# Modulation sums of a diffusion trunk: block turns and row sums on VectorE, a small selection matmul on TensorE

## Chip, cores and metric

The kernel runs on one core of a Trainium2 chip. The metric is the device time of one execution in microseconds (us), the median of several runs. All work is in float32; large products are split into a high and a low part that TensorE multiplies in its faster fp32r form, three matmuls for each product.

## What is computed

The reference is a two-layer trunk over 256 latent and 256 context tokens of width 1024. Each layer has an FFN, a token-mixing part and a second FFN, and each of the three is modulated: nine vectors of 1024 values per layer and stream, computed from a conditioning vector.

```python
sc = jax.nn.silu(c);  scc = jax.nn.silu(c_ctx)
mod_x = (sc @ w_mod[l] + b_mod[l]).reshape(b_, N_MOD, 1, D_MODEL)      # N_MOD = 9
mod_h = (scc @ w_mod[l] + b_mod[l]).reshape(N_MOD, 1, D_MODEL)

def adaln_in(s, g_pre, shift, scale):
    return rmsnorm(s, g_pre) * (1 + scale) + shift
def adaln_out(s, y, g_post, gate, weight):
    return s + weight * gate * rmsnorm(y, g_post)
def swiglu(y, wg, wu, wd):
    return (jax.nn.silu(y @ wg) * (y @ wu)) @ wd
```

For sub-layer j the vectors 3j and 3j + 1 are shift and scale, and 3j + 2 is the gate. The change concerns only how `sc @ w_mod` and `scc @ w_mod` are summed over the 1024 rows of `w_mod`.

## The kernel before

**Modulation.** The first two vectors of layer 0 are made at the start on TensorE (`mod_first`). The other 16 (7 of layer 0, 9 of layer 1) are made in halves of 512 columns, 32 halves in all, by the generator `mod_half` (line 345), while the FFNs run. A half loads its 1024 x 512 part of `w_mod` in two blocks of 1 MB (`stage`, line 207), and VectorE multiplies each 128-row slice by the conditioning value of its row and adds it to one of two accumulators, one for each stream: 16 instructions of 128x512 (lines 355 and 357). What is left is the sum over the 128 partitions. Line 367 makes it on TensorE, with a matrix of ones: four matmuls of 256 columns in four strips of 32 output rows. A gate (q % 3 == 2) is then finished by VectorE at lines 375 and 376 as rows of 256 and written to a table in DRAM by four GpSimd DMAs (line 379); its bias and norm weight come by eight small SyncE DMAs (`by_groups`, line 338). A shift or scale has to be turned so that its 1024 values lie along partitions: ScalarE copies the sums out of PSUM (line 383), and two transposes on TensorE follow later (`turn`, line 385, a "flip"), after which `mod_put` (line 322) writes the coefficients.

**Order of the work.** The program order is laid out by a small planner in the kernel's own source. Its clock `clk` is advanced by `tick(n)` by n / 2400 for n matmul columns; tasks are generators in a heap and run when the clock reaches their due time. `step()` (line 401), called after each pair of hidden blocks of an FFN (line 644) and before each pair of token blocks in the first two down phases (line 494), launches one half when the clock has passed the last launch plus `MOD_PACE`. The half's loads and VectorE work are issued at the next tick, its sums `T_MOD` later. At the start of the last down phase of an FFN, `step(len(modq))` (line 505) launches all that are left in the queue; then `drain` waits for those that are needed next. An FFN has 22 hidden blocks in phases of 6, 8 and 8; each phase is gate/up work for pairs of blocks, then a down projection. The queue gets 12 halves before the first FFN, 10 before the second and 10 before the third; the fourth has none.

**Buffers.** All weight blocks, those of `w_mod` included, pass through three staging buffers (`wst`, tag `stg`). A weight block is split by ScalarE (high part, line 240) and VectorE (low part, line 101) into one of three pairs of buffers (`hi`, `lo`), which TensorE holds until it is done with the block. In the last down phase (from line 505) the two blocks of the first column half are loaded and split ahead of the first matmuls, the two of the second column half after those of the first stream's token blocks in program order. The tile framework places every instruction in its engine's queue by its place in the program and by when its inputs are expected; instructions under `high_priority` go ahead. The two accumulators have the tag `a`, two buffers, so a half can't begin before the one before it is summed.

Of the kernel before, what the change touches and what calls it, by code (L numbers as in the profile page):

```python
# [12 lines left out]
F32 = mybir.dt.float32  # L13
F32R = mybir.dt.float32r
AF = mybir.ActivationFunctionType
ALU = mybir.AluOpType
AX = mybir.AxisListType
PSUM = bass.MemoryType.PSUM

P = 128  # L20
# [15 lines left out]


T_SOFT, T_SOFTC, T_TURN, T_POST = 4.5, 3.5, 1.5, 3.0
T_MOD, T_FLIP, MOD_PACE = 15.0, 2.5, 18.0
PACE_IN, PACE_OUT, PACE_DRAIN = 1.8, 1.0, 1.0  # L40
PACE_IN1, PACE_OUT1, PACE_DRAIN1, T_CHAIN, T_LATE = 1.5, 1.2, 1.2, 7.5, 10.5
PHASES = ((0, 6), (6, 8), (14, 8))
# [21 lines left out]
def trunk(ctx: ExitStack, tc: tile.TileContext, x, c, cx, c_ctx, w_mod, b_mod, norm_pre, norm_post,  # L64
          w_gate, w_up, w_down, w_in, w_out, v_gain, w_s, b_s, diff_lambda, diff_subln, swa_sink,
          rope, out):
    nc = tc.nc

    const = ctx.enter_context(tc.tile_pool(name="const", bufs=1))
# [3 lines left out]
    wk = ctx.enter_context(tc.tile_pool(name="wk", bufs=2))  # L73
    sm = ctx.enter_context(tc.tile_pool(name="sm", bufs=4))
# [6 lines left out]
    def nm(s):  # L81
        cnt[0] += 1
        return f"{s}{cnt[0]}"
# [7 lines left out]
    def pc():  # L91
        return psc.tile([P, 512], F32, tag="c", name=nm("pc"))

    def half(s):
        return wk.tile([P, 512], F32, tag="p", name=nm(s), bufs=6)
# [15 lines left out]
    def run_next():  # L111
        due, _, g = heapq.heappop(evq)
        clk[0] = max(clk[0], due)
        busy[0] = True
        d = next(g, None)
        busy[0] = False
        if d is not None:
            later(d, g)

    def tick(n):  # L120
        clk[0] += n / 2400.0
        while evq and not busy[0] and evq[0][0] <= clk[0]:
            run_next()
# [7 lines left out]

        later(delay, run())

    flips = []

    def flip_now():
        while flips:
            flips.pop(0)()

    def drain(tag):  # L140
        while pending.get(tag, 0):
            run_next()
        if tag[0] == "m":
            flip_now()


    ident = const.tile([P, P], F32, name="ident")
    make_identity(nc, ident)
    ones = const.tile([P, P], F32, name="ones")
    nc.vector.memset(ones, 1.0)  # L150
    negh = const.tile([P, 8], F32, name="negh")
    nc.vector.memset(negh, -0.5)
    mask = const.tile([P, 2, P], F32, name="mask")
# [12 lines left out]
    gtab = {(l, j): dr.tile([2, D], F32, name=f"gate{l}{j}") for l in range(DEPTH) for j in range(3)}  # L166
# [40 lines left out]
    def stage(src_list, nk, ncol, slot="stg"):  # L207
        pool = wst if slot == "stg" else wsp
        st = pool.tile([P, 2048], F32, tag=slot, name=nm(slot))
        v = st[:, 0:nk * ncol].rearrange("p (k c) -> p k c", k=nk)  # L210
        for c0, c1, src in src_list:
            nc.sync.dma_start(v[:, :, c0:c1], src.rearrange("(k p) c -> p k c", p=P))
        return v
# [108 lines left out]
    def mod_put(l, q, b, n, src, mid):  # L322
        j, kind = q // 3, q % 3
        dst = coef[:, l, j, kind, b:b + n, :]

        def bc(ap):
            return ap.unsqueeze(2).to_broadcast([P, n, 2])

        bias = bc(bm[:, l, q * KB + b:q * KB + b + n])
        if kind == 0:  # L330
            nc.vector.tensor_tensor(dst, src, bias, op=ALU.add)
            return
        nc.vector.tensor_tensor(mid, src, bias, op=ALU.add)
        nc.vector.scalar_tensor_tensor(dst, mid, 1.0, bc(npre[:, l, j, b:b + n]),
                                       op0=ALU.add, op1=ALU.mult)


    def by_groups(src):
        r = wk.tile([P, 256], F32, tag="sq", name=nm("gr"), bufs=7)
        for j in range(4):  # L340
            nc.sync.dma_start(r[32 * j:32 * j + 32, :],
                              src[256 * (j % 2):256 * (j % 2) + 256].partition_broadcast(32))
        return r

    def mod_half(l, q, hf):
        acc = [wk.tile([P, 512], F32, tag="a", name=nm("acc")) for _ in range(2)]
        c0 = q * D + hf * 512
        for part in range(2):
            v = stage([(0, 512, w_mod[l, part * 512:(part + 1) * 512, c0:c0 + 512])], 4, 512)
            for k in range(4):  # L350
                kk = 4 * part + k
                for st, a in enumerate(acc):
                    sc = sT[:, kk, st:st + 1]
                    if kk == 0:
                        nc.vector.tensor_scalar(a, v[:, k, :], sc, None, op0=ALU.mult)
                    else:
                        nc.vector.scalar_tensor_tensor(a, v[:, k, :], sc, a, op0=ALU.mult,  # L357
                                                       op1=ALU.add)
        gate = q % 3 == 2
        j = q // 3  # L360
        if gate:
            br = by_groups(b_mod[l, c0:c0 + 512])
            gr = by_groups(norm_post[l, j, hf * 512:(hf + 1) * 512])
        yield T_MOD
        t = pc()
        for i in range(4):
            nc.tensor.matmul(t[32 * i:32 * i + 32, 0:256], lhsT=ones[:, 0:32],
                             rhs=acc[i // 2][:, 256 * (i % 2):256 * (i % 2) + 256],
                             start=True, stop=True, tile_position=(0, 32 * i))
        tick(1024)  # L370
        flip_now()
        if gate:

            w = math.sqrt(D) * (1.0 if j == 1 else 0.5)
            nc.vector.tensor_tensor(br, t[:, 0:256], br, op=ALU.add)
            nc.vector.scalar_tensor_tensor(br, br, w, gr, op0=ALU.mult, op1=ALU.mult)  # L376
            for i in range(4):
                f0 = hf * 512 + 256 * (i % 2)
                nc.gpsimd.dma_start(gtab[l, j][i // 2:i // 2 + 1, f0:f0 + 256],  # L379
                                    br[32 * i:32 * i + 1, :])  # L380
            return
        ev = wk.tile([P, 256], F32, tag="sq", name=nm("modev"), bufs=7)
        nc.scalar.activation(ev, t[:, 0:256], AF.Copy)

        def turn():
            u = pc()
            for i in range(2):
                nc.tensor.transpose(u[:, i * P:(i + 1) * P], ev[:, i * P:(i + 1) * P], ident)
            tick(600)
            uv = u[:, 0:256].rearrange("p (i s h r) -> p h i s r", i=2, s=2, h=2)  # L390
            tmp = sm.tile([P, 2, 2, 2], F32, tag="modt", name=nm("modt"))
            for h in range(2):
                mod_put(l, q, 4 * hf + 2 * h, 2, uv[:, h, :, :, 0], tmp[:, h])

        flips.append(turn)

    modq = []

# [77 lines left out]
    def down(l, e, pi, f0, nf, Z, Uh, Ul, order, nxt):  # L476
# [13 lines left out]
        if not final:  # L490
# [13 lines left out]
            return  # L504
        step(len(modq))
        drain(("m", l, j))
        if nxt is not None:
            drain(("m",) + nxt[:2])
# [46 lines left out]
    def ffn(l, e, streams, nxt, first=None, out_order=None):  # L555
# [36 lines left out]
        for pi, (f0, nf) in enumerate(PHASES):  # L592
            Uh = big.tile([P, KB, NT], F32R, tag="Uh", name=nm("Uh"))
            Ul = big.tile([P, KB, NT], F32R, tag="Ul", name=nm("Ul"))
            for fp in range(0, nf, 2):
# [19 lines left out]
                if two:  # L615
                    into = [t[:, 4:8, :].rearrange("p a (b c) -> p (a b) c", b=2)
                            for t in (Uh, Ul)]
                    second = gate_up(l, e, cs + 256, into, True)
                    for s in range(2) if rows else streams:
                        drain(("y", s))  # L620
                        for f, (g_, u_) in ((0, (wg, wu)), (2, second)):
                            if rows:
                                gu = pa()
                                acc3_multi([(gu[:, c0:c0 + 256], rterms(w, s), c0 == 0)
                                            for w, c0 in ((g_, 0), (u_, 256))])
                                task("u", hidden_rows(gu, f, s))
                                continue
                            gus = [pa(), pa()]
                            groups = []
                            for w, c0 in ((g_, 0), (u_, 256)):  # L630
                                for i in range(2):
                                    groups.append((gus[i][:, c0:c0 + 256], yterms(w, i * P, s),
                                                   c0 == 0))
                            acc3_multi(groups)
                            for i in range(2):
                                hidden(gus[i][:, 0:256], gus[i][:, 256:512], f + i, s)
                else:
                    for i in range(2):
                        g = pa()
                        acc3(g[:, 0:n], yterms(wg, i * P, ys))  # L640
                        u = pa()
                        acc3(u[:, 0:n], yterms(wu, i * P, ys))
                        hidden(g[:, 0:n], u[:, 0:n], fp + i, full)
# [581 lines left out]
    acc, ws0 = {}, {}  # L1225
# [57 lines left out]
    def halves(l, *qs):  # L1283
        for q in qs:
            for hf in range(2):
                modq.append((("m", l, q // 3), mod_half(l, q, hf)))
# [42 lines left out]
```

## Time and profile before

| | |
|---|---|
| median of 3 runs | 1762.15 us (1761.32 to 1762.53) |
| profiled execution | 1762.98 us |
| its span, first to last instruction | 1761.2 us |
| TensorE, matmuls | 1722.4 us, 98% of the span |
| VectorE | 1190.4 us, 68% |
| ScalarE | 696.3 us, 40% |
| mean granted clock of TensorE | 0.997 of full speed |

In the profile PE is TensorE's matmuls, PEld its weight loads, DVE is VectorE, ACT ScalarE, POOL GpSimd and SP SyncE, which issues the loads. L367 is line 367 of the kernel. Matmuls overlap, so a matmul's own duration is longer than its share of the stream; the distance between two starts is what counts. In a timeline a row is a start, a duration, the engine, the line, the operation, the tile written and the tiles read, shapes, and how many instructions are merged in the row; what stands in brackets is how long the engine had been idle and what released it.

### The profile page before, as it was taken

Reading aid. Unit: us, or ns where it says so; the run is one execution under the profiler, and the core shown is the slowest. Engines: PE = TensorE matmul, PEld = TensorE weight load, DVE = VectorE, ACT = ScalarE, POOL = GpSimd, SP = SyncE. Lnnn points to the kernel's source line nnn. Section 1 sums busy time; section 2 is a strip of 40 time slices with the busy share of each in tenths; the row PEclk is TensorE's granted clock in tenths of the full one; section 3 lists DMA queues with packets and bytes.
Section 4 is the critical chain, followed back from the end, with each engine's and each line's share of the span. In section 5 each row is a group of like instructions: output and inputs, shape, how many; then the busy total and the mean of one; then the engine's idle time right before and its main releaser. Section 6 shows DMA issues by size and latency. Waiting matters only on the chain.

```text
span 1761.2 us, 24837 instructions
## 1 busy us (share of the span) xinstructions
PE 1722.4 (98%) x9663; PEld 1449.9 (82%) x9663; DVE 1190.4 (68%) x2174; ACT 696.3 (40%) x1480; POOL 168.9 (10%) x185
## 2 busy tenths in 40 slices
PE   7999999999999999999999999999999999999998
PEld 5788888879977789888888898888888897689997
DVE  4876876775667576768766576777864756765555
ACT  4332322244376562333232442332223526655443
POOL 0000000021322120000000210000001321010000
PEclk9999999999999999999999999999999999999999
DMA  9654554543131143445545233655544133226552
GB/s 336 207 173 160 188 197 144 167 150 109 60 103 52 57 137 125 162 163 189 191 144 185 75 120 123 205 178 191 180 144 167 48 108 120 73 90 197 192 191 84
DMA packets 197105, 259.20 MB, mean 147 GB/s; under 512 B 8234, under 2 KB 132348, under 8 KB 196988
## 3 DMA queue, kind: packets, MB, share of 16 engines
q1 hardware_dynamic: 195452, 257.56, 44.3%
q8 instruction: 76, 1.25, 0.3%
q14 instruction: 41, 0.34, 0.1%
q0 software_dynamic: 1536, 0.05, 0.0%
HBM read 256.49 MB, written 1.10 MB: 146 GB/s over the span
## 4 chain that ended last, share of the span: by engine, by line
PE 63%; DVE 7%; ACT 2%; issue 2%; POOL 1%; DMA 1%; POOLq 0%; DVEq 0%; ACTq 0%
PE pa L250 19%; PE pa L254 9%; PE pb L269 4%; PE pb L271 4%; PE pb L263 4%; PE pa L263 4%; PE pa L271 4%; PE pa L269 4%; PE pb L250 3%; DVE lo L101 2%; PE pb L254 1%; PE pa L797 1%; PE pc L818 1%; PE pc L895 1%; DVE S L439 1%
## 5 line engine op out<-in xcount | busy, mean ns | idle before, releaser
L101 DVE TENSOR_TENSOR lo<-stg,hi 128x512 fp32r<-128x512 f32 (+3 forms) x476 | 367.0, 807 | 192.5 <-ACT hi L240 122.8
L240 ACT ACTIVATE hi<-stg 128x512 fp32r<-128x512 f32 (+3 forms) x496 | 318.4, 702 | 329.6 <-PE pa L263 97.2
L250 PE MATMUL pa<-Yh,hi 128*128 128x512 f32 (+1 forms) x1168 | 415.0, 365 | 0.0
L250 PE MATMUL pa<-Yl,hi 128*128 128x512 f32 (+1 forms) x1168 | 413.8, 364 | 0.0
L357 DVE SCALAR_TENSOR_TENSOR acc<-stg,sT,acc 128x512 f32<-128x512 f32 x448 | 305.2, 743 | 4.0 <-DMA stg<-in_w_mod_dram 4.0
L254 PE MATMUL pa<-Yh,lo 128*128 128x512 f32 (+1 forms) x1168 | 257.8, 363 | 0.0
L250 PEld LDWEIGHTS pa<-Yh,hi 128*128 128x128 f32 x1168 | 220.5, 189 | 36.6 <-issue 2.9
L250 PEld LDWEIGHTS pa<-Yl,hi 128*128 128x128 f32 x1168 | 220.5, 189 | 35.0 <-issue 1.2
L254 PEld LDWEIGHTS pa<-Yh,lo 128*128 128x128 f32 x1168 | 202.4, 189 | 34.3
L570 ACT ACTIVATE Uh<-ha 128x512 fp32r<-128x512 f32 (+1 forms) x92 | 50.7, 551 | 296.4 <-DVE ha L568 296.4
L263 PE MATMUL pb<-hi,Ul 128*128 128x512 f32 x400 | 156.9, 392 | 0.0
L271 PE MATMUL pb<-lo,Uh 128*128 128x512 f32 x400 | 155.9, 390 | 0.8 <-DVE lo L101 0.8
L269 PE MATMUL pb<-hi,Uh 128*128 128x512 f32 x400 | 155.8, 391 | 0.1
L568 DVE TENSOR_TENSOR ha<-ha,pa 128x512 f32<-128x512 f32 (+1 forms) x91 | 53.0, 583 | 79.5 <-PE pa L254 79.0
L269 PE MATMUL pa<-Yh,hi 128*128 128x256 f32 x368 | 92.0, 285 | 0.0
L271 PE MATMUL pa<-Yl,hi 128*128 128x256 f32 x368 | 91.3, 283 | 0.0
L271 PEld LDWEIGHTS pb<-lo,Uh 128*128 128x128 f32 x400 | 75.1, 188 | 16.6 <-DVE lo L101 1.3
L263 PEld LDWEIGHTS pb<-hi,Ul 128*128 128x128 f32 x400 | 75.1, 188 | 16.5 <-issue 1.2
L269 PEld LDWEIGHTS pb<-hi,Uh 128*128 128x128 f32 x400 | 75.2, 188 | 16.0 <-DVE Z L503 0.5
L566 ACT ACTIVATE ht<-pa 128x512 f32<-128x512 f32 (+1 forms) x91 | 46.3, 510 | 104.1 <-PE pa L254 81.8
L379 POOL DMA_DIRECT2D gate<-gr x48 | 24.3, 513 | 603.7 <-DVE gr L376 535.3
L567 DVE SCALAR_TENSOR_TENSOR ha<-ht,pa 128x512 f32<-128x512 f32 (+1 forms) x91 | 52.9, 581 | 37.2 <-ACT ht L566 36.4
(299 smaller groups left out, 2732.4 us busy)
## 6 DMA issues: line engine op xcount, KB each, us to landing
stg<-in_w_mod_dram SPq DMA_DIRECT2D x64, 1024.0 KB, 5.0
stg<-in_ffn_w_gate_dram SPq DMA_DIRECT2D x42, 1024.0 KB, 5.2
stg<-in_ffn_w_up_dram SPq DMA_DIRECT2D x42, 1024.0 KB, 5.1
stg<-in_ffn_w_down_dram SPq DMA_DIRECT2D x32, 1024.0 KB, 5.0
stg<-in_w_in_dram SPq DMA_DIRECT2D x14, 1024.0 KB, 4.8
stg<-in_ffn_w_down_dram SPq DMA_DIRECT2D x16, 768.0 KB, 4.4
mst<-in_w_mod_dram SPq DMA_DIRECT2D x16, 512.0 KB, 7.6
stg<-in_w_out_dram SPq DMA_DIRECT2D x8, 1024.0 KB, 6.4
```

The lines of the kernel that those rows point to most:

```text
L101: eng.tensor_tensor(lo, full, f32(hi), op=ALU.subtract)
L240: nc.scalar.activation(hi[:, a:b, :], v[:, a:b, :], AF.Copy)
L250: nc.tensor.matmul(o, lhsT=ah, rhs=r, start=(i == 0), stop=(i == n - 1))
L254: nc.tensor.matmul(o, lhsT=al, rhs=bh, start=(i == 0), stop=(i == n - 1))
L263: nc.tensor.matmul(o, lhsT=al, rhs=bh, start=False, stop=last, skip_group_check=True)
L269: nc.tensor.matmul(o, lhsT=ah, rhs=bh, start=(first and k == 0), stop=False, skip_group_check=True)
L271: nc.tensor.matmul(o, lhsT=ah, rhs=bl, start=False, stop=False, skip_group_check=True)
L357: nc.vector.scalar_tensor_tensor(a, v[:, k, :], sc, a, op0=ALU.mult, op1=ALU.add)
L566: nc.scalar.activation(t, g, AF.Tanh, scale=0.5)
L567: nc.vector.scalar_tensor_tensor(a, t, 1.0, g, op0=ALU.add, op1=ALU.mult)
L568: nc.vector.tensor_tensor(a, a, u, op=ALU.mult)
L570: nc.scalar.activation(uh, a, AF.Copy)
```

## The change

Each accumulator of 128x512 is turned on VectorE in blocks of 32x32, and its rows are summed in groups of 32. That leaves, for each stream, 16 columns in which a partition holds the sum over one group of 32 of the original partitions; only four partial sums remain. A matrix `sel` (128x32, the identity summed over its four groups) adds these four on TensorE. For a shift or scale the result comes out along partitions, four matmuls of 8 columns, and `mod_put` is called once for four blocks, straight from PSUM: the ScalarE copy and the flips are gone, with the list that held them and `flip_now`, which also ticked inside `drain`. For a gate one matmul gives a 32x32 tile, 16 rows for each stream, and the bias, the norm weight and the table write go by 16x32 tiles: two small loads for each in place of four, two writes in place of four. The sum and flip ticks of 1024 and 600 become one of 600; `T_MOD` goes from 15 to 20 and `MOD_PACE` from 18 to 22.

```diff
-T_MOD, T_FLIP, MOD_PACE = 15.0, 2.5, 18.0
+T_MOD, T_FLIP, MOD_PACE = 20.0, 2.5, 22.0
...
     def drain(tag):
         while pending.get(tag, 0):
             run_next()
-        if tag[0] == "m":
-            flip_now()
...
-    ones = const.tile([P, P], F32, name="ones")
-    nc.vector.memset(ones, 1.0)
+    sel = const.tile([P, 32], F32, name="sel")
+    nc.vector.tensor_reduce(sel, ident.rearrange("p (g j) -> p j g", g=4), axis=AX.X, op=ALU.add)
...
     def by_groups(src):
-        r = wk.tile([P, 256], F32, tag="sq", name=nm("gr"), bufs=7)
-        for j in range(4):
-            nc.sync.dma_start(r[32 * j:32 * j + 32, :],
-                              src[256 * (j % 2):256 * (j % 2) + 256].partition_broadcast(32))
+        r = sm.tile([32, 32], F32, tag="gr", name=nm("gr"))
+        for st in range(2):
+            nc.sync.dma_start(r[16 * st:16 * st + 16, :], src.rearrange("(b c) -> b c", c=32))
         return r
...
+        sums = sm.tile([P, 2, 16], F32, tag="sums", name=nm("sums"))
+        for st, a in enumerate(acc):
+            turned = half("mt")
+            nc.vector.transpose(turned, a)
+            nc.vector.tensor_reduce(sums[:, st, :], turned.rearrange("p (b i) -> p b i", i=32), axis=AX.X,
+                                    op=ALU.add)
         yield T_MOD
         t = pc()
-        for i in range(4):
-            nc.tensor.matmul(t[32 * i:32 * i + 32, 0:256], lhsT=ones[:, 0:32],
-                             rhs=acc[i // 2][:, 256 * (i % 2):256 * (i % 2) + 256],
-                             start=True, stop=True, tile_position=(0, 32 * i))
-        tick(1024)
-        flip_now()
         if gate:
+            nc.tensor.matmul(t[0:32, 0:32], lhsT=sums.rearrange("p s b -> p (s b)"), rhs=sel,
+                             start=True, stop=True)
+            tick(600)
...
-            nc.vector.tensor_tensor(br, t[:, 0:256], br, op=ALU.add)
+            nc.vector.tensor_tensor(br, t[0:32, 0:32], br, op=ALU.add)
             nc.vector.scalar_tensor_tensor(br, br, w, gr, op0=ALU.mult, op1=ALU.mult)
-            for i in range(4):
-                f0 = hf * 512 + 256 * (i % 2)
-                nc.gpsimd.dma_start(gtab[l, j][i // 2:i // 2 + 1, f0:f0 + 256],
-                                    br[32 * i:32 * i + 1, :])
+            for st in range(2):
+                nc.gpsimd.dma_start(gtab[l, j][st, hf * 512:(hf + 1) * 512]
+                                    .rearrange("(b c) -> b c", c=32), br[16 * st:16 * st + 16, :])
             return
-        ev = wk.tile([P, 256], F32, tag="sq", name=nm("modev"), bufs=7)
-        nc.scalar.activation(ev, t[:, 0:256], AF.Copy)
-        def turn():
...
-        flips.append(turn)
+        sv = sums.rearrange("p s (b m) -> p s b m", m=4)
+        for m in range(4):
+            nc.tensor.matmul(t[32 * m:32 * m + 32, 0:8], lhsT=sel, rhs=sv[:, :, :, m], start=True,
+                             stop=True, tile_position=(0, 32 * m))
+        tick(600)
+        tmp = sm.tile([P, 4, 2], F32, tag="modt4", name=nm("modt"))
+        mod_put(l, q, 4 * hf, 4, t[:, 0:8].rearrange("p (s b) -> p b s", s=2), tmp)
```

## Rows read from the trace of the kernel before

**Rows 1.** The page's first part: busy time of each engine.

```profile
PE 1722.4 (98%) x9663; PEld 1449.9 (82%) x9663; DVE 1190.4 (68%) x2174; ACT 696.3 (40%) x1480; POOL 168.9 (10%) x185
```

**Rows 2.** Timeline of TensorE around the sums of a gate half.

```profile
79.26 1.07 PE L254 MATMUL pa<-Yh,lo 128*128 128x512 f32 x4
80.25 0.64 PE L367 MATMUL pc<-acc,ones 128*32 128x256 f32 x8
81.16 0.39 PE L250 MATMUL pa<-Yl,hi 128*128 128x512 f32 x1
```

**Rows 3.** Timeline of TensorE: sums of another half, and the next sums.

```profile
190.52 1.98 PE L254 MATMUL pa<-Yh,lo 128*128 128x512 f32 x8
192.43 0.64 PE L367 MATMUL pc<-acc,ones 128*32 128x256 f32 x8
...
193.51 0.39 PE L250 MATMUL pa<-Yl,hi 128*128 128x512 f32 x1
...
215.16 0.64 PE L367 MATMUL pc<-acc,ones 128*32 128x256 f32 x8
```

**Rows 4.** Timeline of TensorE: two transposes put between matmuls of a down phase.

```profile
370.13 0.39 PE L263 MATMUL pb<-hi,Ul 128*128 128x512 f32 x1
370.36 0.38 PE L683 MATMUL pc<-ident,wr 128*128 128x128 f32 x2
...
370.85 0.40 PE L271 MATMUL pb<-lo,Uh 128*128 128x512 f32 x1
```

**Rows 5.** Groups by line and shape, VectorE: busy us, mean ns, idle before.

```profile
L800 DVE TENSOR_REDUCE mx<-pa 128x1 f32<-128x512 f32 x32 | 21.4, 684 | 3.2 <-PE pa L797 3.0
...
L704 DVE STREAM_SHUFFLE shf<-QK 128x256 f32<-128x256 f32 x16 | 6.4, 447 | 0.0
...
L471 DVE CAST Yh<-yf 128x512 fp32r<-128x512 f32 x36 | 22.1, 617 | 12.9 <-ACT yf L466 12.7
```

**Rows 6.** Timeline of VectorE: one half's first multiply and its multiply-adds.

```profile
114.82 0.49 DVE L355 TENSOR_SCALAR acc<-stg,sT 128x512 f32<-128x512 f32 x1 [2.21 <-PE pc L367]
...
116.33 9.35 DVE L357 SCALAR_TENSOR_TENSOR acc<-stg,sT,acc 128x512 f32<-128x512 f32 x14
```

**Rows 7.** Who waited for whom: us in total, times, longest us.

```profile
DVE acc L355 <- PE pc L367: 30.4, 9, 5.8
```

**Rows 8.** Timelines of ScalarE, VectorE and TensorE, first FFN's last down phase.

```profile
356.72 2.01 ACT L240 ACTIVATE hi<-stg 128x1024 fp32r<-128x1024 f32 x2 [5.37 <-DMA stg<-in_ffn_w_down_dram]
...
360.37 3.39 DVE L357 SCALAR_TENSOR_TENSOR acc<-stg,sT,acc 128x512 f32<-128x512 f32 x5
...
363.95 1.22 DVE L101 TENSOR_TENSOR lo<-stg,hi 128x1024 fp32r<-128x1024 f32 x1
...
363.25 1.20 PE L367 MATMUL pc<-acc,ones 128*32 128x256 f32 x8 [0.38 <-DVE acc L357]
365.22 0.50 PE L271 MATMUL pb<-lo,Uh 128*128 128x512 f32 x1 [0.78 <-DVE lo L101]
```

**Rows 9.** Second FFN's end, by stretch: length; PE, PEld, DVE, ACT, POOL busy; clock; DMA.

```profile
951.80:973.70 21.90, 21.90 (x100) 18.11 (x98) 8.59 (x10) 6.50 (x9) 0.00 (x0) 1.00 0.49 165
973.70:984.60 10.90, 10.90 (x51) 9.04 (x49) 6.78 (x11) 3.42 (x6) 1.28 (x1) 1.00 0.78 265
984.60:995.50 10.90, 10.90 (x50) 9.03 (x49) 3.73 (x7) 2.84 (x8) 2.18 (x2) 1.00 0.05 19
```

**Rows 10.** Timelines of SyncE and VectorE, second FFN: down weights loaded and split.

```profile
955.60 0.39 SPq L212 DMA_DIRECT2D stg<-in_ffn_w_down_dram  x1
...
968.35 1.23 DVE L101 TENSOR_TENSOR lo<-stg,hi 128x1024 fp32r<-128x1024 f32 x1 [3.42 <-PE pa L254]
...
974.61 1.23 DVE L101 TENSOR_TENSOR lo<-stg,hi 128x1024 fp32r<-128x1024 f32 x1
```

**Rows 11.** The same view, two stretches near the start of the kernel.

```profile
18.00:21.00 3.00, 1.60 (x12) 1.17 (x14) 2.26 (x9) 2.33 (x5) 0.00 (x0) 0.98 1.09 385
21.00:25.00 4.00, 4.00 (x13) 2.60 (x14) 3.78 (x8) 0.84 (x2) 0.00 (x0) 0.59 1.08 392
```

More of the change, by code (lines that the diff above doesn't have):

```diff
@@ L132, in task @@
         later(delay, run())
[L134 to L138, printed above, removed]
     def drain(tag):
@@ L381, in mod_half @@
             return
-        ev = wk.tile([P, 256], F32, tag="sq", name=nm("modev"), bufs=7)
-        nc.scalar.activation(ev, t[:, 0:256], AF.Copy)
-        def turn():
[L386 to L393, printed above, removed]
```

## The prediction

> **What bounds the kernel now.** I read the page's engine table first: TensorE is busy 98% of the span, VectorE 68% [rows 1]. Then the timeline of TensorE inside a gate/up block, to see whether that 98% is work or waiting. A 512-column matmul starts every 0.227 us (eight take 1.98 us from 190.52, the last one 0.39 of it: 1.59 / 7) [rows 3, 4], without a hole, and the sums of two successive halves stand 22.7 us apart, 215.16 - 192.43 [rows 3]. Four groups of 24 matmuls make 96 x 0.227 = 21.8 us, and the sums and flips account for the other 0.9. So in this stretch TensorE is the bound, and whatever is taken out of its stream comes off the end time; VectorE has idle time. The profiled execution took 1762.98 us (span 1761.2 and 1.8 around it), 0.8 above the median of 1762.15; I sum against the former and carry the difference over to the median.
>
> **What leaves TensorE.** There are 32 halves (16 modulation vectors, two halves each): 12 gates, 20 others. A gate half: four matmuls of the line before it run from 79.26, so the next slot is 79.26 + 4 x 0.227 = 80.17; instead the second 512-column matmul after the sums starts at 81.16, where 80.17 + 0.227 was due: 0.76 us [rows 2]. Another half, with the flips of the one before beside it: 190.52 + 8 x 0.227 = 192.34, second matmul at 193.51: 0.94 us [rows 3]. Total 12 x 0.76 + 20 x 0.94 = 27.9 us.
>
> **What enters TensorE.** A gate half issues one small fp32 matmul, another half four into four column strips. None of these is in the trace. The cheapest insertion seen is a pair of 128-column fp32 passes: 370.85 - 370.13 - 2 x 0.227 = 0.27 us [rows 4]. The dearest reasonable one is a little under what is there now, say 0.6: the same four strips with the same number of passes, only shorter. I take 0.3 for a gate and 0.4 for another half, since most of 0.27 is the change between kinds of matmul, not columns: 12 x 0.3 + 20 x 0.4 = 11.6 us. **Gain on TensorE: 27.9 - 11.6 = 16 us** (9 at 0.6 each, 19 at 0.27 each).
>
> **What enters VectorE.** Per half two 32x32-block turns and two row sums of 128x512. Nearest rows: a reduction of 128x512 takes 684 ns, a shuffle of half that width 447 ns, a cast of 128x512 617 ns on average [rows 5]. I take 0.65 each, 2.6 us a half; bounds 1.8 (0.45 each, as if the full width cost what the shuffle's half does) and 3.6 (twice that). The multiply-adds of a half are 14 in 9.35 us, and two first multiplies of 0.49, of which the next instruction overlaps a little: 0.45 each [rows 6]; 10.2 us. A half is then 12.8 us of VectorE (12.0 to 13.8), and 32 x 2.6 = 83 us are added in all. The shorter gate arithmetic and the halved number of table writes give back some tenths per half; the ScalarE copy (20 times), half of the SyncE and GpSimd DMAs of the gates and the large gate tiles go too. No queue of those sets the end, so I cost them at nothing; they are hidden under TensorE's matmuls, and would cost their few tenths each if these were not there. One rule of the Trainium skill speaks against this trade (VectorE: DVE Perf Modes, Rules for kernel authors): a row reduction is the slowest kind of operation on that engine and should be kept off a busy path. By the rows here it is hardly slower than its neighbours: 684 ns [rows 5] against 9.35 / 14 = 0.67 us for a multiply-add [rows 6].
>
> A wait goes as well: VectorE stood 30.4 us, 9 times, before the first multiply of a half until TensorE had summed the previous one [rows 7]. The accumulators are now freed by VectorE itself. Inside a gate/up block this shortens nothing, since TensorE did not wait for VectorE there.
>
> **What the new pace moves.** This is the part that decides. A half is launched at a step (after each pair of hidden blocks, or before a pair of token blocks in a down phase) when the planner's clock has passed the last launch plus MOD_PACE. One gate/up block ticks 4 x 24 x 512 / 2400 = 20.48; with the ticks of a half (0.43 + 0.25 before, 0.25 after) a step comes every 21.16 before and 20.73 after. Before, 21.16 is over 18, so each step launches. After, 20.73 is under 22, so **every second step launches**. In the down phases steps come every 7.68 or 10.24: the third still qualifies (23.0, 30.7). Counting through the steps with the code's ticks: the first FFN launches 8 of its 12 halves in pace (before 12), the second and the third 7 of 10 (before 10). The last down phase of each FFN then calls step(len(modq)) and launches what is left: **4, 3 and 3 halves at once**. They are issued at the first tick, hence after the two weight blocks of the first column half and ahead of the two of the second; they take the same three staging buffers and the same VectorE.
>
> Does VectorE take such a half ahead of later weight splits? The first FFN's last half did fall into its last down phase. ScalarE had the next weight block's high part ready from 356.72 + 2.01 = 358.7, but VectorE ran five more multiply-adds from 360.37 and came to that block's low part only at 363.95; TensorE waited for it [rows 8]. So yes, and one late half cost about 1.2 us (0.78 there and 0.38 before its sum).
>
> Now three halves. In the second FFN the last block's matmuls end and the down phase begins at 973.7; VectorE is busy 8.6, 6.8 and 3.7 us in the three stretches to 995.5 [rows 9]. The four weight blocks were all issued by 955.60, and two of them were already staged long before their split (968.35, 974.61) since the split waits for a pair buffer that TensorE holds [rows 10]. So the queued halves find a free staging buffer only when the first block's split is over, about 952. From there VectorE owes 3 x 12.8 = 38.4 us and its other work up to 995.5, 19.1 less four half-block splits of 1.2 [rows 10] that now stand behind: 14.3. The first split of the third block ends near 952 + 38.4 + 14.3 + 1.2 = 1006. TensorE has 10.9 us of work on the first two blocks and, if the other stream's token blocks are drawn ahead, another 10.9: until 995.5. It stands 10 us, and again in the third FFN; with four halves 12.8 + 2 more, 25 us. **Loss 10 + 10 + 25 = 45 us.** Without drawing ahead TensorE is out of work at 984.6: 21 + 21 + 36 = 78 us. If the halves get buffers 10 us earlier, the loss is 0 + 0 + 15.
>
> **Forecast.** 1762.98 - 16 + 45 = 1792 for the profiled execution, 1791 on the median's footing.
>
> **Rivals.**
> *Backlog absorbed, faster.* With no wait for TensorE before a half, VectorE may run all queued halves in its idle time. It decides when VectorE has finished the backlog by 995.5 in the second FFN, that is some 10 us earlier than I find, and 25 in the first. For it: VectorE's idle share before 973.7 (8.6 busy of 21.9) [rows 9]. Against: the staging buffers hold weights then. Time 1762 - 16 = 1746 (1743 to 1753).
> *Nothing drawn ahead, slower still.* The program order of token blocks is kept: 1762 - 16 + 78 = 1824.
> *TensorE gains nothing.* The change of matmul kind is the whole of the 0.76 to 0.94, and the small matmuls cost as much: 1762 + 45 = 1807. Against: a pair of passes inserted for 0.27 [rows 4].
> *Both small*, 1763: gain 9 and loss about the same.
> A stall may also cost clock. At the start of this trace TensorE was busy 1.60 us of three (18 to 21), and the granted clock of the next four was 0.59, between the two levels of 1.2 and 2.4 GHz [rows 11]; four such microseconds lose 4 x 0.41 = 1.6 us per stall, 5 in all, inside the range. The Trainium skill (TensorE: Matmul & The Clock Gate, Why this matters for your kernels) warns against idle gaps between matmul bursts for this reason; the rows at the start agree, and none later in this trace shows such a drop.
>
> **How the numbers follow.** Forecast 0.45 (its own range 1768 to 1812), nothing drawn ahead 0.20, absorbed 0.23, TensorE gains nothing 0.05, both small 0.07. What a measurement tells from no change is 0.2%, 3.5 us. Slower 0.45 + 0.20 + 0.05 = 0.70, less 0.02 for the corner where the forecast's bounds all turn out low, which goes to faster: 0.68 and 0.23 + 0.02 = 0.25; same 0.07. The range runs from 1746, in the absorbed case, to 1826.
>
> **What the profile will show.** Right or wrong, step by step: sums in the gate/up blocks 43 to 44 us apart instead of 22.7; their insertion 0.3 to 0.4 us; turns and row sums of 0.4 to 0.9 us; three or four halves of multiply-adds in an unbroken run at the start of each last down phase; TensorE idle there, released by the low part of a weight split. If TensorE shows no hole there, the loss is wrong and the absorbed case holds. If each sum still costs 0.7 or more, the gain is wrong.

## The result, and the profile after

The changed kernel takes 1815.36 us (1814.56 to 1817.7) beside 1762.22 us of the kernel before on the same chip: a ratio of 1.0306, slower by 53 us; the 95% interval of the ratio is [1.0291, 1.0322], and brackets behind a ratio mean this below too. The page of the changed kernel, its span, TensorE's and VectorE's busy time, and in 40 slices TensorE's busy share and granted clock:

```profile
span 1813.0 us, 24539 instructions
...
PE 1714.9 (95%) x9551; PEld 1453.0 (80%) x9551; DVE 1261.7 (70%) x2272; ACT 690.6 (38%) x1460; POOL 158.2 (9%) x161
...
PE   7999999939999999999999699999997899999998
...
PEclk9999999969999999999999799999999899999999
```

Beside [rows 1], TensorE works 7.5 us less (1722.4 - 1714.9) and stands 59.3 us more: its span less its busy time is 98.1 us now, 38.8 before. Between the start and the end, the standing is in three places (the digits 3, 6 and 78 in the row PE), and there the clock dips too. They are the last down phases of the three FFNs. Who waited for whom in TensorE's case (us in total, times, longest):

```profile
PE pb L264 <- DVE lo L101: 25.7, 3, 8.7
PE pb L262 <- ACT hi L233: 22.7, 3, 15.9
PE pc L379 <- DVE sums L361: 10.4, 2, 5.2
...
PE pc L366 <- DVE sums L361: 5.2, 1, 5.2
```

That is 64.0 us: 29.6 in the first FFN, 17.2 in each of the others. One of the three places, the second FFN, on VectorE, SyncE and TensorE, and what SyncE's loads wait for from 985 to 1020:

```profile
972.23 0.88 DVE L347 TENSOR_SCALAR acc<-stg,sT 128x512 f32<-128x512 f32 x2
...
1004.56 1.29 DVE L360 STREAM_TRANSPOSE mt<-acc 128x512 f32<-128x512 f32 x2
1005.78 1.24 DVE L361 TENSOR_REDUCE sums<-mt 128x16 f32<-128x512 f32 x2
1006.94 0.87 DVE L347 TENSOR_SCALAR acc<-stg,sT 128x512 f32<-128x512 f32 x2
1007.73 9.36 DVE L349 SCALAR_TENSOR_TENSOR acc<-stg,sT,acc 128x512 f32<-128x512 f32 x14
1017.00 1.29 DVE L360 STREAM_TRANSPOSE mt<-acc 128x512 f32<-128x512 f32 x2
1018.22 1.23 DVE L361 TENSOR_REDUCE sums<-mt 128x16 f32<-128x512 f32 x2
1019.38 2.35 DVE L101 TENSOR_TENSOR lo<-stg,hi 128x1024 fp32r<-128x1024 f32 x2
...
1004.67 0.37 SPq L205 DMA_DIRECT2D stg<-in_ffn_w_down_dram  x1
SPq L205 <- DVE acc L349: 27.1, 4, 9.1
...
990.69 0.39 PE L262 MATMUL pb<-hi,Uh 128*128 128x512 f32 x1
...
1001.69 0.25 PE L379 MATMUL pc<-sums,sel 128*32 128x8 f32 x8
1007.16 0.30 PE L379 MATMUL pc<-sums,sel 128*32 128x8 f32 x8 [5.23 <-DVE sums L361]
1010.75 1.22 PE L262 MATMUL pb<-hi,Uh 128*128 128x512 f32 x2 [3.28 <-ACT hi L233]
1020.64 0.79 PE L264 MATMUL pb<-lo,Uh 128*128 128x512 f32 x1 [8.68 <-DVE lo L101]
```

The phase begins at 990.69. From 1006.94 VectorE does nothing but a left-over half, without a break, and only then the low part of the weight block that TensorE needs. That block's load was issued at 1004.67, behind the halves' own loads: they hold the staging buffers, and a buffer comes free only when VectorE's multiply-adds are through with it; in the kernel before, the last of these was issued at 955.60, 18 us ahead of the phase [rows 9, 10]. The sums of the first left-over half (1001.69) find their input ready. Then TensorE stands for the sums of the second (5.2), then for the block's high part (3.3), then, behind the third half, for its low part (8.7).

What the change was to save is there. Inside gate/up blocks the sums of a gate half and of another half now look so on TensorE's timeline:

```profile
83.98 1.75 PE L247 MATMUL pa<-Yh,lo 128*128 128x512 f32 x7
85.66 0.25 PE L366 MATMUL pc<-sel,sums 128*32 128x32 f32 x2
...
86.18 0.39 PE L243 MATMUL pa<-Yh,hi 128*128 128x512 f32 x1
...
143.50 0.39 PE L243 MATMUL pa<-Yl,hi 128*128 128x512 f32 x1
143.82 0.25 PE L379 MATMUL pc<-sums,sel 128*32 128x8 f32 x8
...
144.34 0.39 PE L243 MATMUL pa<-Yl,hi 128*128 128x512 f32 x1
```

The gate half: 83.98 + 8 x 0.227 = 85.80 was due, 86.18 came: 0.38 us, where [rows 2] had 0.76. The other: 143.50 + 2 x 0.227 = 143.95 was due, 144.34 came: 0.39, where [rows 3] had 0.94. And the sums are twice as far apart as in [rows 3], 217.85 - 173.92 = 43.9 us instead of 22.7:

```profile
173.92 0.25 PE L379 MATMUL pc<-sums,sel 128*32 128x8 f32 x8
...
217.85 0.25 PE L379 MATMUL pc<-sums,sel 128*32 128x8 f32 x8
```

### The profile page after: what moved, and what is told of

The parts are those of the page before. It is cut to its first block, busy times and chain, and to the rows that moved or that the text cites. A ratio compares the mean times of both kernels' runs of the same rounds, so it can differ in the third digit from the quotient of the medians.

```text
span 1813.0 us, 24539 instructions
## 1 busy us (share of the span) xinstructions
PE 1714.9 (95%) x9551; PEld 1453.0 (80%) x9551; DVE 1261.7 (70%) x2272; ACT 690.6 (38%) x1460; POOL 158.2 (9%) x161
## 4 chain that ended last, share of the span: by engine, by line
PE 81%; DVE 11%; ACT 3%; issue 2%; DMA 1%; POOL 1%; POOLq 0%; DVEq 0%; ACTq 0%; SPq 0%
PE pa L243 26%; PE pa L247 13%; PE pb L264 5%; PE pb L262 5%; PE pb L256 5%; PE pa L256 5%; PE pa L262 5%; PE pa L264 5%; DVE acc L349 3%; PE pb L243 3%; DVE lo L101 2%; PE pb L247 1%; PE pa L1242 1%; PE pa L785 1%; PE pc L806 1%
## 5 line engine op out<-in xcount | busy, mean ns | idle before, releaser
L349 DVE SCALAR_TENSOR_TENSOR acc<-stg,sT,acc 128x512 f32<-128x512 f32 x448 | 310.3, 754 | 5.6 <-DMA stg<-in_w_mod_dram 5.5
L247 PE MATMUL pa<-Yh,lo 128*128 128x512 f32 (+1 forms) x1168 | 262.1, 365 | 0.0
L243 PEld LDWEIGHTS pa<-Yl,hi 128*128 128x128 f32 x1168 | 220.7, 189 | 34.4
L243 PEld LDWEIGHTS pa<-Yh,hi 128*128 128x128 f32 x1168 | 220.5, 189 | 34.1
L262 PE MATMUL pb<-hi,Uh 128*128 128x512 f32 x400 | 159.6, 401 | 22.8 <-ACT hi L233 22.7
L264 PEld LDWEIGHTS pb<-lo,Uh 128*128 128x128 f32 x400 | 76.7, 192 | 43.7 <-DVE lo L101 27.9
L264 PEld LDWEIGHTS pa<-Yl,hi 128*128 128x128 f32 x368 | 70.7, 192 | 0.1
L262 PEld LDWEIGHTS pa<-Yh,hi 128*128 128x128 f32 x368 | 70.6, 192 | 0.1
```

What stands on the lines that cost most here:

```text
L243: nc.tensor.matmul(o, lhsT=ah, rhs=r, start=(i == 0), stop=(i == n - 1))
L247: nc.tensor.matmul(o, lhsT=al, rhs=bh, start=(i == 0), stop=(i == n - 1))
L262: nc.tensor.matmul(o, lhsT=ah, rhs=bh, start=(first and k == 0), stop=False, skip_group_check=True)
L264: nc.tensor.matmul(o, lhsT=ah, rhs=bl, start=False, stop=False, skip_group_check=True)
```

## The experiments

Theory A: the time is lost by the pace alone. MOD_PACE 22 is just over a step's 20.73, so every second step launches nothing, and the 4, 3 and 3 left-over halves run in a row on VectorE ahead of the weight splits of the second column half. Rival B: VectorE's added 83 us of turns and row sums are what delays TensorE. All ratios are to the kernel before on the same chip.

| kernel | median us | ratio [interval] |
|---|---|---|
| new sums, old pace | 1744.67 | 0.9899 [0.9885, 0.9914] |
| old sums, new pace | 1860.91 | 1.0563 [1.0545, 1.0581] |
| changed, pace 20.7 | 1742.05 | 0.9886 [0.9871, 0.9901] |
| changed, pace 20.8 | 1815.80 | 1.0302 [1.0287, 1.0317] |
| changed, weights first | 1839.44 | 1.0431 [1.0416, 1.0447] |
| changed, turns twice | 1847.23 | 1.0474 [1.0456, 1.0492] |
| changed, both streams first | 1808.10 | 1.0248 [1.0231, 1.0265] |
| weights first, pace 20.7 | 1746.91 | 0.9902 [0.9886, 0.9917] |
| turns twice, pace 20.7 | 1745.94 | 0.9909 [0.9889, 0.9928] |

**New sums, old pace.** The changed kernel with the constants of the kernel before.

```diff
-T_MOD, T_FLIP, MOD_PACE = 20.0, 2.5, 22.0
+T_MOD, T_FLIP, MOD_PACE = 15.0, 2.5, 18.0
```

> The changed kernel with T_MOD and MOD_PACE back at 15 and 18; new sums, no flips. Theory A (the loss is the halves that the slower pace leaves for the last down phases): with a step every 20.73 and a pace of 18 every step launches, nothing is left over, TensorE's idle time there is gone, and what remains is the gain of the sums: 1762 - 13 to 1762 - 16, that is 1746 to 1750 us. Theory B (the loss is the 83 us of block turns and row sums themselves, which make VectorE late): a half in every gate/up block asks VectorE for 8.6 + 12.8 = 21.4 of some 22.1 us, so it gets worse, over 1815 us.

1744.67 us, 17.2 faster than the kernel before, a little more than expected. The sums, with all of VectorE's 83 us, are a gain when each step launches a half. Rival B falls here as a cause by itself.

**Old sums, new pace.** The kernel before with the constants of the changed one.

```diff
-T_MOD, T_FLIP, MOD_PACE = 15.0, 2.5, 18.0
+T_MOD, T_FLIP, MOD_PACE = 20.0, 2.5, 22.0
```

> The kernel before with T_MOD 20 and MOD_PACE 22 alone; old sums, flips kept. A half's ticks make a step come every 21.16, still under 22. Theory A: halves are left over as in the changed kernel, and the last down phases stall: 1762 + 50 to 1762 + 75 = 1812 to 1837 us (a half is 10.2 us of VectorE in place of 12.7, but each has to wait for TensorE's sum of the one before). Theory B: VectorE has no more work than before, so 1762 within 4 us.

1860.91 us: 99 lost, more than I expected and more than the 74 that the pace costs the new sums (below). Here TensorE's waits, and VectorE at the start of the second FFN's last down phase:

```profile
PE pc L367 <- DVE acc L357: 65.8, 9, 10.2
...
1001.53 0.48 DVE L355 TENSOR_SCALAR acc<-stg,sT 128x512 f32<-128x512 f32 x1 [4.40 <-PE pc L367]
```

The first left-over half waits here for its accumulators, until TensorE has summed the half before (1001.53). With the new sums the first left-over half of that phase ran from 972.23 to 990.45, in the idle time of the last gate/up block, ahead of the phase's start at 990.69. So the wait of [rows 7], which I had said shortens nothing, does matter once halves are queued: the changed kernel starts its backlog one half earlier. That this is the whole of the 25 us between 99 and 74 was not tested by itself.

**Pace 20.7 and pace 20.8.** A step ticks 20.73, so 20.7 launches at each step and 20.8 at every second; nothing else differs.

```diff
-T_MOD, T_FLIP, MOD_PACE = 20.0, 2.5, 22.0
+T_MOD, T_FLIP, MOD_PACE = 20.0, 2.5, 20.7
```

> The changed kernel with MOD_PACE 20.7 and T_MOD 20. A gate/up block with one half ticks 20.48 + 0.25 = 20.73, so each step just qualifies. Theory A: like the pace of 18, 1746 to 1752 us. Theory B: over 1815 us, as at 18.

> The changed kernel with MOD_PACE 20.8 and T_MOD 20, a tenth above the run before. Theory A: 20.73 no longer qualifies, every second step launches, halves are left over: within 10 us of 1815. Theory B, or any cause that grows smoothly with the pace: within 5 us of the run with 20.7.

1742.05 us, a little below the range expected, and 1815.80: 0.1 in a constant is worth 73.7 us, and 20.8 is as slow as 22. At 20.7 the page and the sums on TensorE's timeline read:

```profile
span 1742.8 us, 24544 instructions
...
PE 1706.9 (98%) x9551; PEld 1447.8 (83%) x9551; DVE 1258.5 (72%) x2272; ACT 690.0 (40%) x1460; POOL 156.0 (9%) x161
...
172.52 0.25 PE L379 MATMUL pc<-sums,sel 128*32 128x8 f32 x8
...
194.69 0.25 PE L379 MATMUL pc<-sums,sel 128*32 128x8 f32 x8
```

The sums stand 22.2 us apart, VectorE is as busy as in the changed kernel (1258.5 to 1261.7), and TensorE stands 35.9 us in all (1742.8 - 1706.9). At 20.8 the span is 1814.2 with TensorE busy 1715.2: 63.1 us more standing and 8.3 more busy, which makes the 71.4 us between the two spans. The version with 20.7 beats both kernels.

**Weights first.** Pace 22; the weight blocks of both column halves are issued before the phase's first matmuls, ahead of the left-over halves.

```diff
-                if s == order[0]:
-                    into = None
...
-                    ws[hf] = [chunk(hf, 0), chunk(hf, 1, into)]
+                if s == order[0] and not hf:
+                    for h in range(2):
...
+                        ws[h] = [chunk(h, 0), chunk(h, 1, into)]
```

> The changed kernel, pace 22 as it stands, but in the last down phase of each FFN the weight blocks of the second column half are loaded and split ahead of the first matmuls, with those of the first, so that they are queued on SyncE, ScalarE and VectorE ahead of the 4, 3 and 3 left-over halves. Theory A (the loss is TensorE standing for a weight split that waits behind the left-over halves; 64 us of idle time in three places): most of the hole goes, 1752 to 1777. Rival (VectorE has too much work in this stretch, in whatever order it comes): 1805 to 1816, with the idle time moved to another place.

1839.44 us, worse, and outside of what either theory gave. The hole did leave the phase: its down matmuls in the first FFN now run from 350.61 to 399.01, 48.4 us, against 79.0 in the changed kernel. It came back right behind it. TensorE's longest waits are now as follows; the first of them, in the first FFN, is shown on VectorE and TensorE:

```profile
PE pc L379 <- DVE coef L324: 23.4, 1, 23.4
PE pa L262 <- DVE Yh L459: 18.6, 3, 8.1
PE pc L366 <- DVE modt L326: 16.3, 1, 16.3
...
420.88 1.27 DVE L361 TENSOR_REDUCE sums<-mt 128x16 f32<-128x512 f32 x2
422.07 0.22 DVE L324 TENSOR_TENSOR coef<-pc,bm 128x8 f32<-128x8 f32 x2
...
422.37 0.44 PE L379 MATMUL pc<-sums,sel 128*32 128x8 f32 x16 [23.36 <-DVE coef L324]
```

Put behind the weights, the last of the first FFN's four was summed on VectorE by 422.15 instead of 391.35. Its loads stood behind weight blocks that waited for pair buffers, so VectorE left 13 us between 332 and 351 unused, and later it did the tokens' residuals between the halves. With `coef` and `modt` VectorE empties TensorE's two sum tiles (`pc`); here it does so only behind the last half's row sums. The sums of the last two halves wait for that, and the next stage's matmuls stand behind these sums in TensorE's queue. So the order of the weights alone is no cure: whichever goes first, TensorE stands for the other. By the order in which the program queues them (the calls of `halves` at the end of the kernel), all left-over vectors belong to the sub-layer after the next. TensorE thus stands here for sums that nothing in this stretch needs; what placing them later would give was not tested. My rival was right that the idle time moves to another place, and expected no loss where 24 us were lost.

**Turns twice, pace 22 and pace 20.7.** Each half's turns and row sums are done a second time.

```diff
-            nc.vector.transpose(turned, a)
-            nc.vector.tensor_reduce(sums[:, st, :], ...)
+            for _ in range(2):
+                nc.vector.transpose(turned, a)
+                nc.vector.tensor_reduce(sums[:, st, :], ...)
```

> The changed kernel, pace 22, with each half's turns and row sums done twice (the second time to the same result). Theory A: VectorE's chain of the 10 left-over halves is on the path, and each grows by 2.45 us (four instructions at a pitch of 0.61 us in the changed kernel's trace): +24, so 1839 (1832 to 1845); the other 22 halves cost nothing, 54 us on VectorE beside other work. Rival (the stall is set by the loads of the modulation's weights, or by TensorE's own queue): 1815 to 1820. If VectorE's whole work counted, 32 halves would add 78: 1893.

> Turns and row sums done twice, at pace 20.7, where every step launches a half and nothing is left over. Theory A (VectorE's work counts only where left-over halves run in series ahead of TensorE's next matmul): 32 x 2.45 = 78 us more on VectorE, all of it beside TensorE: 1742 to 1750, against 1742.05 without. Rival (VectorE has little slack once each step carries a half, so longer halves delay the gates and up-products): half of the 78 or more shows, 1780 or later.

At pace 22, 1847.23 us, just above the range expected: 31.9 more. At pace 20.7, 1745.94: 3.9 more, for the same VectorE work, and there the intervals of the two ratios overlap. TensorE's waits at pace 22:

```profile
PE pb L264 <- DVE lo L101: 39.9, 3, 13.4
PE pc L380 <- DVE sums L362: 24.5, 2, 12.3
PE pb L262 <- ACT hi L233: 18.0, 3, 15.9
PE pc L367 <- DVE sums L362: 12.3, 1, 12.3
```

These are the same four waits as in the changed kernel (the edit moves lines 361, 366 and 379 down by one), 94.7 us instead of 64.0. So VectorE's work counts where halves run in a row, and nearly nowhere else. The 24.5 us that ten halves give is short of the 31.9 by about one half per FFN. By FFN the waits are 41.5, 26.6 and 26.6 us instead of 29.6, 17.2 and 17.2: 11.9, 9.4 and 9.4 more, near five, four and four times 2.45. So the half just before the left-over ones seems to count too.

**Both streams first.** Pace 22; the last down phase does the first column half of both streams before the second column half, so that TensorE has 10.9 us more of work in hand before it needs the late weights. This is the case that my forecast had assumed.

```diff
-        for s in order:
...
-            for hf in range(2):
+        for hf in range(2):
...
+            for s, own, st, gp, ss in parts:
```

> The changed kernel, pace 22, with the loops of the last down phase exchanged: the first column half of both streams, then the second column half of both. TensorE then has the other stream's token blocks (10.9 us of matmuls) to do before it needs the second column half's weights. Theory A with my figure for nothing drawn ahead (each of the three stalls is the left-over chain less what TensorE still has to do): 3 x 10.9 less, 1783 (1778 to 1793). Rival (TensorE stands at the sum of a left-over half wherever it comes in its queue, so more blocks ahead of the weights help nothing): 1810 to 1818.

1808.10 us: 7 less, of the 33 expected, and just below my rival's range. From the first to the last down matmul the three phases take 71.5, 56.2 and 61.3 us instead of 79.0, 66.5 and 67.4: 24 us less. But from the end of each to the next anchor (the next FFN's first down matmul, or the last one of all) it is 8.9, 5.2 and 6.4 us longer, 20.5 together. After the second phase, by stretch (columns as in [rows 9]):

```profile
1047.00:1050.00 3.00, 0.26 (x3) 0.02 (x1) 1.45 (x3) 2.48 (x7) 0.00 (x0) 1.00 0.00 0
1050.00:1057.00 7.00, 6.71 (x30) 6.45 (x31) 6.52 (x14) 5.70 (x14) 3.04 (x3) 0.51 0.01 2
1057.00:1064.00 7.00, 7.00 (x62) 7.00 (x61) 6.55 (x13) 4.17 (x10) 0.87 (x1) 1.00 0.09 21
```

The residuals of all token blocks now fall at the end of the phase; the next stage's first matmul waits for its input, and then TensorE runs seven microseconds at a granted clock of 0.51: 30 matmuls, against 62 in the same length at 1.00.

**Weights first at pace 20.7.** The edit of the weights-first kernel, and:

```diff
-T_MOD, T_FLIP, MOD_PACE = 20.0, 2.5, 22.0
+T_MOD, T_FLIP, MOD_PACE = 20.0, 2.5, 20.7
```

> Pace 20.7 as in the best run so far (1742.05) and the second column half's weights loaded early as well. Theory A: nothing is left over at pace 20.7, so the order of the weights has nothing to hide: 1740 to 1744. Rival (the early loads crowd VectorE at the start of the phase, when it has the first half's blocks to split): 1745 to 1755.

1746.91 us (1742.03 to 1747.41). That is in my rival's range, but its interval and that of pace 20.7 alone overlap: no gain, and a small loss can't be told from none.

## Why the prediction was right, and where it was not

- **The sign and the mechanism**: right. Every second step launches (43.9 us between sums), the rest is left over, and TensorE stands in the three last down phases, released by a weight split, and also by the sums of left-over halves, which the prediction did not name. The two paces 0.1 apart on either side of 20.73 show that the threshold is the cause. That 4, 3 and 3 halves are left shows in the sums on TensorE behind the start of each last down phase (in the second FFN at 1001.69, 1007.16 and 1033.11). The unbroken run at the start of the phase is right only in part: the first left-over half begins before the phase (972.23), the second runs between other work, and only the rest run unbroken.
- **Gain on TensorE, 16 us**: right. By the rows, 32 insertions of 0.38 make 12.2 us where 11.6 was assumed, so 27.9 - 12.2 = 15.7. At pace 20.7 TensorE's busy time is 15.5 us below that of [rows 1], and the idle time 2.9 lower.
- **A half on VectorE, 12.8 us**: right, and for the right reason. Turns and row sums follow each other at 0.61 us (1004.56 to 1005.78 is two of them), so 2.45 a half where I took 2.6, and the half from 1006.94 to 1019.38 is 12.4.
- **When the backlog ends**: right within 3 us. I had the first late split end near 1006 in the frame of the kernel before; its second FFN's phase starts at 973.7 [rows 9], the changed kernel's at 990.69, 17.0 later; so 1023, and 1020.6 was measured.
- **When TensorE runs out of work**: wrong, and this is the step that failed. I chose the case in which the other stream's token blocks are drawn ahead (995.5), with a loss of 45 us. In the trace TensorE comes to the sums of a left-over half at 1001.69, which is 984.6 + 17.0 and 0.1: nothing is drawn ahead, and TensorE keeps the order of the program, sums of left-over halves included. That was my rival with 36, 21 and 21 us, 78 in all and 1824. Measured are 29.6, 17.2 and 17.2 of standing, 64.0, and 73.7 as the whole price of the pace. The time alone would not tell this: it lies outside the forecast's own range (1768 to 1812), 9 below this rival and 8 above the one in which TensorE gains nothing (1807), which falls with the 15.5 us above. The sum with 78 gives 1825 for the profiled execution, 10 above the 1814.83 measured: TensorE stands 14.0 less in these phases and 4.7 less elsewhere, and is busy 8.5 longer than 1722.4 - 16 (the sum had no term for the clock). The program order of the phase, first stream through both column halves before the second stream, would have told this without a trace.
- **Drawing ahead as a remedy**: had I been right on the order, the loss would still not have been 45. The run that puts both streams first got the hole 24 us smaller and gave 20.5 back behind the phase. My sum had no term for what becomes late next.
- **The wait of [rows 7]**: costed at nothing, in a stretch where that holds. With halves queued it delays the first left-over half, as the old sums at the new pace show; how much of their 25 us it explains is open.
- **Clock**: 1.6 us per stall was the estimate. In the second FFN seven starts take 2.99 us after the stall (1021.23 to 1024.22) where 7 x 0.227 = 1.59 was due, and the one before them 0.59 instead of 0.23: 1.8 us. In the whole kernel TensorE is busy 8.3 us longer at pace 20.8 than at 20.7 with the same 9551 matmuls, where the estimate was 5.

The granted clock around the stall, by stretch, and the matmuls behind it on TensorE's timeline:

```profile
1007.00:1011.00 4.00, 0.55 (x9) 0.49 (x10) 4.00 (x8) 1.36 (x2) 0.00 (x0) 0.50 0.51 199
1011.00:1021.00 10.00, 1.32 (x3) 0.60 (x4) 10.00 (x16) 2.64 (x3) 0.00 (x0) 0.50 0.52 172
1021.00:1025.00 4.00, 4.00 (x11) 3.15 (x11) 3.31 (x6) 0.00 (x0) 0.00 (x0) 0.56 1.00 342
...
1021.23 0.63 PE L256 MATMUL pb<-hi,Ul 128*128 128x512 f32 x1
1021.66 0.63 PE L262 MATMUL pb<-hi,Uh 128*128 128x512 f32 x1
...
1024.59 0.39 PE L264 MATMUL pb<-lo,Uh 128*128 128x512 f32 x1
1024.82 0.40 PE L256 MATMUL pb<-hi,Ul 128*128 128x512 f32 x1
```

VectorE is busy for every microsecond of the first two rows while TensorE is busy 0.55 of 4 and 1.32 of 10. The clock is at the lower of its two levels, and matmuls start every 0.43 us until 1024.2, then every 0.23 again.

## What to carry to other kernels

When a change alters the ticks of a step, compare the new step with every threshold that decides what a step may launch: 20.73 against 22 cost 73.7 us here, and 20.7 instead makes the change a gain of 1.1%. Then ask what becomes of the work that isn't launched in pace: where it is emitted, in the program's order, ahead of what, and whether anything in that stretch needs it yet. An engine that is idle for 30% of the span can still be what all others wait for during a few stretches (29.6, 17.2 and 17.2 us here). Moving work within such a stretch (weights first, both streams first) moved most of the wait here and did not remove it.

## What the runs showed of the hardware

- **A turn of 32x32 blocks costs what other passes over 128x512 cost.** Mean durations in the changed kernel: 689 ns for a turn, 660 for a row sum, 754 for a multiply-add.

```profile
L349 DVE SCALAR_TENSOR_TENSOR acc<-stg,sT,acc 128x512 f32<-128x512 f32 x448 | 310.3, 754 | 5.6 <-DMA stg<-in_w_mod_dram 5.5
...
L360 DVE STREAM_TRANSPOSE mt<-acc 128x512 f32<-128x512 f32 x64 | 41.8, 689 | 0.0
L361 DVE TENSOR_REDUCE sums<-mt 128x16 f32<-128x512 f32 x64 | 40.1, 660 | 0.0
```

  The Trainium skill (VectorE: DVE Perf Modes, Rules for kernel authors) calls the row reduction the slowest kind; by these rows it is not slower than the others here.
- **Small matmuls of another kind cost 0.38 us per place, not per matmul, in the two places shown.** One fp32 matmul of 32 columns (two rows in the trace) and four of 8 columns in four strips (eight rows) delay the stream of fp32r matmuls by 0.38 and 0.39 us.
- **A short gap can be dearer than its length.** With both streams first, 3 us with TensorE busy for 0.26 were followed by 7 us at a granted clock of 0.51, in which 30 matmuls were done where the next 7 us did 62: about half of these 7 us was lost besides the gap. The Trainium skill (TensorE: Matmul & The Clock Gate, Why this matters for your kernels) warns of such gaps, and the rows agree.
